# A two-layer attention and retention trunk: later query and key projection blocks held behind a score chunk by a one-element copy, and spread over heads 0 to 5

## The chip, the cores and the metric

The kernel runs on one core of a Trainium2 chip. A core has five engines that run side by side and meet at semaphores: TensorE for matrix products (PE in the profile, with its weight loads as PEld), VectorE (DVE), ScalarE (ACT), GpSimd (POOL), and SyncE (SP), which here issues nearly all DMA transfers. Each engine works through its own queue in order. The metric is device time of one execution in microseconds (us). Before the change the median of three runs is 2404.4 us (2401.87 to 2405.06).

## What is computed

Two layers, each a token mixer followed by a squared-ReLU MLP, both with a residual and a layer norm. The mixer has eight forgetting-attention heads of width 64 and four retention heads. The change lies in the attention heads alone:

```python
def fox_attention(q, k, v, log_f):
    c = jnp.cumsum(log_f.astype(jnp.float32), axis=1).transpose(0, 2, 1)
    ...
        scores = jnp.einsum('bqhd,bkhd->bhqk', q_i, k).astype(jnp.float32) * scale
        bias = c_i[..., :, None] - c[..., None, :]
        ...
        logits = jnp.where(causal, scores + bias, -jnp.inf)
        p = jax.nn.softmax(logits, axis=-1)
        return jnp.einsum('bhqk,bkhd->bqhd', p.astype(v.dtype), v)
```

There are 1024 tokens of width 1024. q, k and v are slices of one projection of the layer's input.

## The kernel before

Products that need full float32 accuracy are made of three: each operand is split into a high and a low part (`split`, L159: ScalarE makes the high part, VectorE the low one), and `mm3` (L229) issues low x high, high x low and high x high.

A layer runs in stages: value projections, retention, attention, output projection, and the two MLP products. Around the change:

**Projection blocks.** `project_qk(l, p, ...)` (L469) makes the queries and keys of a pair of heads, 2p and 2p+1. It yields four blocks: queries of tokens 0 to 511, queries of 512 to 1023, keys of 0 to 511, keys of 512 to 1023. A block is 8 x 3 matmuls of 128 rows by 512 columns into one PSUM bank of the pool `ps_mm` (two banks, tile `mm`), then an eviction (`ev`: one ScalarE and one VectorE instruction) and two stores to the DRAM buffers `q_d` or `k_d`. The generator yields after each k step and after each eviction, so a pair is 36 steps (`QK_STEPS`). Pair 0 is projected before the attention stage. Pairs 1 to 3, the twelve later blocks (called blocks 1 to 12 here: block 4 ends pair 1, block 8 pair 2, block 12 pair 3), are made inside it, by `rest()` (L699), followed by eight transposes of the retention output (`ret_transposes`).

**Attention.** A head has four steps qq = 0 to 3, each of two blocks of 128 query rows. `load(h)` (L498) fetches a head's queries `qs`, keys `ks` (four transfers) and values `vp` back from DRAM; `load_bias(h)` fetches the cumulative gate sums `ncb` (one buffer), and `bias` (POOL, `rel`) turns them into a bias for each step. `front` (L525) computes the scores of a step in chunks of up to 512 keys: two matmuls `qk<-ks,qs` into a bank of `ps_qk` (two banks), a causal mask added on the diagonal (`qk<-mbf,ibf`), then one VectorE instruction that adds the bias, writes `sc` and leaves the running row minimum `mx` (L547); after a row block's last chunk the exponential (ACT, L553), a reciprocal `ri` (DVE) and the scaling by it (POOL, L556). `back` (L560) transposes the probabilities (`tr<-cst,sc`, TensorE) and splits them into `pt` (ACT and DVE); `values` multiplies them with the head's values (`pv<-pt,vp`).

**Order.** In the program the front runs two steps ahead of the back (`DEPTH`), and `merge` interleaves back, front and n steps of `rest()`. n comes from `FILL[h]`, the number of steps a head gets, shared out in proportion to qq + 1. `need(p)` runs what is missing of pairs 1 to p at once. In the main loop step qq = 0 calls `need` (for odd heads) and `load(h+1)`; step qq = 1 calls `load_bias(h+1)`. This is not the order on the chip: the framework plays the whole program against a modelled timeline and gives each engine an instruction as soon as it counts it as ready. A projection block depends on nothing but its input, its weights and a free bank, so it may move far ahead of its place in the program. Once the order is made, an engine keeps to it and waits where something is late.

Of the kernel before, what the change touches and what calls it, by code (L numbers as in the profile page):

```python
# [46 lines left out]
PT_BUFS = 3  # L47
DEPTH = 2
LAG = 5
FILL = (18, 18, 18, 18, 18, 18, 4, 4)  # L50
QK_STEPS = 36


# [22 lines left out]
def hybrid_trunk(ctx: ExitStack, tc, x, w_in, w_out, w_ff1, w_ff2, ln1_g, ln1_b, ln2_g, ln2_b,  # L76
                 b_forget, ret_gn_g, cst_d, rope_d, out):
    nc = tc.nc
    A, V, G, PE, SP = nc.scalar, nc.vector, nc.gpsimd, nc.tensor, nc.sync
# [27 lines left out]
    def small(shape, tag, bufs=2):  # L107
        return sp.tile(shape, F32, tag=tag, name=nm(tag), bufs=bufs)
# [14 lines left out]
    def nm(s):  # L123
        uid[0] += 1
        return f"{s}_{uid[0]}"
# [18 lines left out]
    def tick():  # L144
        now = []
        for it in waiting:
            it[0] -= 1
            if it[0] <= 0:
                now.append(it)
        for it in now:  # L150
            waiting.remove(it)
        for it in now:
            it[1]()
# [5 lines left out]
    def split(hi, lo, src, scale=1.0):  # L159
        if scale == 1.0:  # L160
            A.copy(hi, src)  # L161
            V.tensor_tensor(lo, src, hi.bitcast(F32), op=ALU.subtract)  # L162
        else:
            A.mul(hi, src, scale)
            V.scalar_tensor_tensor(lo, src, scale, hi.bitcast(F32), op0=ALU.mult, op1=ALU.subtract)
# [58 lines left out]
    def weight(*key):  # L224
        while emitted[0] < min(ends[key[0]], place[key] + 1 + AHEAD):
            load_next()
        return loaded.pop(key)

    def mm3(ps, lhs, rhs, ks, first=True, last=True):  # L229
        n = len(ks)  # L230
        for i, k in enumerate(ks):
            for j, (a, b) in enumerate(((1, 0), (0, 1), (0, 0))):
                PE.matmul(ps, lhs(a, k), rhs(b, k), start=first and i == 0 and j == 0,  # L233
                          stop=last and i == n - 1 and j == 2)
# [231 lines left out]
            G.tensor_tensor(gt, gt, gn[:, 256 * r : 256 * r + 256], op=ALU.mult)  # L466
            defer(2, lambda tt=tt, vt=vt, gt=gt: core(tt, vt, gt))

    def project_qk(l, p, xT, pool=None):  # L469
        for name, dst, scale in (("fq", q_d, FD**-0.5), ("fk", k_d, 1.0)):  # L470
            w = weight(l, name, p)
            for hf in range(2):
                ps = ps_mm.tile([P, 512], F32, tag="mm", name=nm("mm"))
                for k in range(8):
                    mm3(ps, lambda a, k: w[a][:, k, :], lambda b, k: xT.at(b, k, 512 * hf, 512), [k], k == 0, k == 7)
                    yield
                if pool is not None and hf == 1:
                    ev = pool.tile([P, 2, 512], F32R, tag="ev2", name=nm("ev"), bufs=1)
                else:
                    ev = wp.tile([P, 2, 512], F32R, tag="ev", name=nm("ev"), bufs=1)  # L480
                split(ev[:, 0, :], ev[:, 1, :], ps, scale)
                for a in range(2):
                    SP.dma_start(dst[2 * p + a, :, :, 512 * hf : 512 * hf + 512].rearrange("s d n -> d s n").bitcast(F32),
                                 ev[64 * a : 64 * a + 64].bitcast(F32))
                tick()
                yield
# [5 lines left out]
            transpose_in(mr, t, tt, groups=1)  # L492
            yield

    def attention(pool, mixes, fill, need, take):
        pv, heads, sums, rels, pvq, outs = {}, {}, {}, {}, [], {}

        def load(h):  # L498
            qs = pool.tile([P, S], F32R, tag="qs", name=nm("qs"), bufs=2)
            SP.dma_start(qs.bitcast(F32), q_d[h].rearrange("s d n -> (s d) n").bitcast(F32))  # L500
            ks = []
            for part in range(2):
                kt = pool.tile([P, S], F32R, tag=f"ks{part}", name=nm("ks"), bufs=2)
                for a in range(2):
                    SP.dma_start(kt[64 * a : 64 * a + 64].bitcast(F32), k_d[h, part].bitcast(F32))
                ks.append(kt)
            vp = pool.tile([P, NT, P], F32R, tag="vp", name=nm("vp"), bufs=2)
            SP.dma_start(vp.bitcast(F32), v_d[:, h].rearrange("(t p) s d -> p t (s d)", p=P).bitcast(F32))
            heads[h] = (qs, ks, vp)
# [15 lines left out]
        def front(h, qq, probs):  # L525
            qs, ks, _ = heads[h]
            n = 256 * (qq + 1)
            rel = rels.pop((h, qq))
            for rb in (2 * qq, 2 * qq + 1):
                ne = (rb + 1) * P  # L530
                sc = pool.tile([P, n], F32, tag=f"sc{qq}", name=nm("sc"), bufs=2)
                mx = None
                nw = max(ne, 256)
                cw = 512 if nw <= 512 or nw % 256 == 0 else nw // 2
                for c0 in range(0, nw, cw):
                    w = min(cw, nw - c0)
                    we = min(w, ne - c0)
                    ps = ps_qk.tile([P, 512], F32, tag="qk", name=nm("qk"))
                    last = c0 + w == nw
                    for part in range(2):  # L540
                        PE.matmul(ps[:, 0:w], qs[:, rb * P : rb * P + P], ks[part][:, c0 : c0 + w],  # L541
                                  start=part == 0, stop=part == 1 and not last)
                    if last:
                        o = rb * P - c0
                        PE.matmul(ps[:, o : o + P], ibf, mbf, start=False, stop=True)
                    m2 = small([P, 1], "mx", 6)
                    V.tensor_tensor_reduce(out=sc[:, c0 : c0 + we], in0=ps[:, 0:we], in1=rel[:, c0 : c0 + we], scale=-1.0,  # L547
                                           scalar=BIG if mx is None else mx, op0=ALU.add, op1=ALU.min, accum_out=m2)
                    mx = m2
                    if not last:  # L550
                        yield
                sm = small([P, 1], "sm", 4)
                A.activation(sc[:, 0:ne], sc[:, 0:ne], AF.Exp, bias=mx, scale=-1.0, accum_out=sm)  # L553
                ri = small([P, 1], "ri", 4)
                V.reciprocal(ri, sm)  # L555
                G.tensor_scalar(sc[:, 0:ne], sc[:, 0:ne], ri, 1.0, op0=ALU.mult, op1=ALU.mult)  # L556
                probs.append(sc)
                yield
# [61 lines left out]
        def fronts(st, probs):  # L620
            h, qq = st
            return (2 * (1 + qq // 2), front(h, qq, probs))
# [8 lines left out]
        for i, st in enumerate(steps):  # L631
            h, qq = st
            n = fill(h, qq)
            if h + 1 < FH:
                if qq == 0:
                    if h % 2 == 1:
                        need((h + 1) // 2)
                    load(h + 1)
                if qq == 3 - DEPTH:
                    load_bias(h + 1)  # L640
            gens = [(2 * (qq + 1), back(h, qq, probs[st]))]
            if i + DEPTH < len(steps):
                nx = steps[i + DEPTH]
                gens.append(fronts(nx, probs[nx]))
            if n:
                gens.append((n, take(n)))
            merge(gens)
            if i + DEPTH + 1 < len(steps):
                bias(*steps[i + DEPTH + 1])
# [3 lines left out]
    def layer(l, xT, nxt):  # L653
# [42 lines left out]
        mix = {}  # L696
        mr = Tokens(act, "act")
        with tc.tile_pool(name=f"p2_{l}", bufs=1, reuse_waits="tile") as pool:
            def rest():  # L699
                for p in range(1, FH // 2):  # L700
                    yield from project_qk(l, p, xT, pool)
                yield from ret_transposes(mr, pool)

            work = rest()

            done = [0, 0.0]

            def fill(h, qq):
                done[1] += FILL[h] * (qq + 1) / 10
                return max(0, int(done[1]) - done[0])  # L710

            def take(n):
                for _ in range(n):
                    done[0] += 1
                    next(work, None)
                    yield

            def need(p):
                while done[0] < QK_STEPS * p:
                    done[0] += 1  # L720
                    next(work, None)

            attention(pool, mix, fill, need, take)
            for _ in work:
                pass

# [10 lines left out]
        with tc.tile_pool(name=f"p3_{l}", bufs=1, reuse_waits="tile") as outer:  # L737
# [3 lines left out]
            with tc.tile_pool(name=f"p3a_{l}", bufs=1, reuse_waits="tile") as pool:  # L741
# [42 lines left out]
                ps = banks(1) + banks(0)  # L784
# [9 lines left out]
                for tt in range(NT):  # L794
                    ps = bank()
# [193 lines left out]
    class Operands:  # L989
# [36 lines left out]
        def take(self, p, j):  # L1026
            self.ahead(self.todo.index((p, j)) + 1 + E_AHEAD)
            return self.ready.pop((p, j))
# [118 lines left out]
    xT = Tokens(act, "act")  # L1147
    for l in range(L):
        nxt = Tokens(act, "act") if l + 1 < L else None
        layer(l, xT, nxt)  # L1150
        xT = nxt
# [27 lines left out]
```

## Time and profile before

| | us |
|---|---|
| median of three runs | 2404.4 |
| the profiled execution, its time | 2406.83 |
| the profiled execution, span of its instructions | 2404.8 |
| attention stage, layer 0: first score matmul to last value matmul | 313.8 to 518.7 |
| attention stage, layer 1 | 1504.7 to 1707.7 |
| granted TensorE clock, mean of the run | 0.997 |

The span is the time from the first to the last instruction; 2.0 us of the execution lie around it. In rows of groups the columns are line, engine, operation, destination and source tiles, shapes and count, then busy time and mean duration, then idle time before the instructions and what ended it. In a timeline row the first two numbers are start and duration in us, the number after x counts merged instructions, and brackets give idle time before the row and its releaser. Window rows give the stretch, its length, and for each engine busy us and instruction count, then the granted clock, the DMA share and GB/s. A matmul's end is modelled: a matmul shown as busy may be held up.

### The profile page before, as it was taken

How to read it: one execution, taken by the hardware profiler on the slowest of the kernel's cores; microseconds unless marked ns; L12 is line 12 of the kernel's file. 1: busy time of each engine (PE TensorE's matmuls, PEld its weight loads, DVE VectorE, ACT ScalarE, POOL GpSimd, SP SyncE). 2: the span in 40 equal slices, each digit the busy share in tenths (PEclk: the TensorE clock that was granted, in tenths of full speed). 3: DMA queues.
4: the chain of work that ended last, by engine and by line, in shares of the span. 5: the costliest groups of instructions: out<-in, count | busy, mean ns of one | idle time of the engine just before them, and what ended most of it. 6: DMA issues, size and time to landing. Idle time of an engine off the chain costs nothing.

```text
span 2404.8 us, 32463 instructions
## 1 busy us (share of the span) xinstructions
PE 2361.1 (98%) x11888; PEld 1983.0 (82%) x11888; DVE 1510.0 (63%) x2703; ACT 1015.2 (42%) x1556; POOL 337.0 (14%) x469
## 2 busy tenths in 40 slices
PE   8999999999999999999999999999999999999997
PEld 8888887887888888888898888888888888888886
DVE  4655447854876667665755554588467766676557
ACT  3222246735544553434321212477274444543331
POOL 0223223500000000000202322244000000000003
PEclk9999999999999999999999999999999999999999
DMA  7465676433364458667555567664334544586664
GB/s 233 165 220 207 216 212 183 123 119 113 109 221 148 145 188 310 211 210 223 179 164 187 209 212 231 182 177 116 132 101 147 199 164 148 213 294 214 196 194 145
DMA packets 243807, 442.47 MB, mean 184 GB/s; under 512 B 26032, under 2 KB 128432, under 8 KB 235456
## 3 DMA queue, kind: packets, MB, share of 16 engines
q1 hardware_dynamic: 241344, 432.01, 55.2%
q10 hardware_dynamic: 2304, 8.39, 0.9%
q8 instruction: 94, 1.54, 0.3%
q14 instruction: 65, 0.53, 0.1%
HBM read 301.85 MB, written 138.48 MB: 183 GB/s over the span
## 4 chain that ended last, share of the span: by engine, by line
PE 88%; DMA 4%; DVE 4%; ACT 1%; issue 1%; SPq 0%; POOL 0%; DVEq 0%; ACTq 0%; POOLq 0%
PE mm L233 17%; PE qk L233 11%; PE qk L860 9%; PE tr L1070 7%; PE pv L1070 7%; PE pv L860 7%; PE qk L1070 5%; PE mm L1070 5%; PE mm L860 5%; PE tr L860 4%; PE tr L569 2%; PE qk L541 2%; PE pv L591 2%; DMA q_d<-ev 1%; PE pv L233 1%
## 5 line engine op out<-in xcount | busy, mean ns | idle before, releaser
L162 DVE TENSOR_TENSOR elo<-est,ehi 128x1024 fp32r<-128x1024 f32 x216 | 261.2, 1222 | 180.3 <-ACT ehi L161 179.4
L161 ACT CAST ehi<-est 128x1024 fp32r<-128x1024 f32 x216 | 226.7, 1054 | 343.4 <-PE pv L1070 127.5
L233 PE MATMUL mm<-whi,act 128*128 128x512 f32 (+1 forms) x608 | 187.9, 375 | 0.9 <-DVE act L162 0.5
L233 PE MATMUL qk<-whi,act 128*128 128x512 f32 (+1 forms) x608 | 186.6, 373 | 0.8 <-DVE act L162 0.8
L860 PE MATMUL qk<-xop,whi 128*128 128x512 f32 x608 | 187.3, 389 | 0.0
L161 ACT CAST whi<-wst 128x512 fp32r<-128x512 f32 (+1 forms) x140 | 115.9, 830 | 165.8 <-PE qk L233 36.0
L286 POOL TENSOR_SCALAR sd<-mv 128x1 f32<-128x1 f32 x15 | 13.9, 928 | 1211.4 <-DVE mv L283 1211.0
L860 PE MATMUL pv<-xop,whi 128*128 128x512 f32 x512 | 157.7, 389 | 0.0
L162 DVE TENSOR_TENSOR wlo<-wst,whi 128x512 fp32r<-128x512 f32 (+1 forms) x140 | 132.0, 946 | 39.2 <-ACT whi L161 38.6
L860 PEld LDWEIGHTS qk<-xop,whi 128*128 128x128 f32 x608 | 114.2, 188 | 23.6
L162 DVE TENSOR_TENSOR pt<-tr,pt 128x512 fp32r<-128x512 f32 (+1 forms) x160 | 99.7, 631 | 46.5 <-ACT pt L161 45.8
L233 PEld LDWEIGHTS mm<-whi,act 128*128 128x128 f32 x608 | 112.6, 192 | 19.7 <-ACT whi L161 0.8
L591 PE MATMUL pv<-pt,vp 128*128 128x256 f32 (+1 forms) x640 | 127.5, 302 | 0.2
L233 PE MATMUL mm<-act,whi 128*128 128x512 f32 x384 | 125.9, 396 | 0.0
L233 PEld LDWEIGHTS qk<-whi,act 128*128 128x128 f32 x608 | 110.3, 189 | 18.7 <-DVE act L162 1.0
L553 ACT ACTIVATE sc<-sc,mx 128x128 f32<-128x128 f32 (+7 forms) x128 | 99.4, 777 | 51.9 <-DVE mx L547 44.4
L860 PE MATMUL mm<-xop,whi 128*128 128x512 f32 x384 | 118.6, 390 | 1.5 <-DVE xop L162 1.5
L860 PE MATMUL qk<-xop,wlo 128*128 128x512 f32 x304 | 118.6, 390 | 0.0
L556 POOL TENSOR_SCALAR sc<-sc,ri 128x128 f32<-128x128 f32 (+7 forms) x128 | 96.8, 762 | 136.7 <-DVE ri L555 104.8
L161 ACT CAST pt<-tr 128x512 fp32r<-128x512 f32 (+1 forms) x160 | 85.8, 541 | 70.0 <-PE tr L569 67.9
L233 PE MATMUL mm<-wlo,act 128*128 128x512 f32 (+1 forms) x304 | 113.7, 374 | 0.7 <-DVE wlo L162 0.7
L860 PEld LDWEIGHTS pv<-xop,whi 128*128 128x128 f32 x512 | 96.1, 188 | 20.0
(278 smaller groups left out, 5942.8 us busy)
## 6 DMA issues: line engine op xcount, KB each, us to landing
est<-h_d SPq DMA_DIRECT2D x224, 256.0 KB, 3.6
wst<-in_w_ff_dram SPq DMA_DIRECT2D x76, 512.0 KB, 4.3
wr<-in_w_ff_dram SPq DMA_DIRECT2D x32, 1024.0 KB, 5.1
t_d<-ts SPq DMA_DIRECT2D x32, 1024.0 KB, 4.2
h_d<-hs SPq DMA_DIRECT2D x32, 1024.0 KB, 5.5
est<-t_d SPq DMA_DIRECT2D x128, 256.0 KB, 4.0
h_d<-rest SPq DMA_DIRECT2D x32, 768.0 KB, 5.7
est<-in_w_ff_dram SPq DMA_DIRECT2D x96, 256.0 KB, 4.8
```

Source lines behind the costliest of these rows:

```text
L161: A.copy(hi, src)
L162: V.tensor_tensor(lo, src, hi.bitcast(F32), op=ALU.subtract)
L233: PE.matmul(ps, lhs(a, k), rhs(b, k), start=first and i == 0 and j == 0, stop=last and i == n - 1 and j == 2)
L286: G.tensor_scalar(sd, mv[:, :, 1], EPS, 1.0, op0=ALU.add, op1=ALU.mult)
L541: PE.matmul(ps[:, 0:w], qs[:, rb * P : rb * P + P], ks[part][:, c0 : c0 + w], start=part == 0, stop=part == 1 and not last)
L553: A.activation(sc[:, 0:ne], sc[:, 0:ne], AF.Exp, bias=mx, scale=-1.0, accum_out=sm)
L556: G.tensor_scalar(sc[:, 0:ne], sc[:, 0:ne], ri, 1.0, op0=ALU.mult, op1=ALU.mult)
L569: PE.transpose(tr[:, 2 * i + rb, :], probs[rb][:, j * P : j * P + P], ident)
L591: PE.matmul(ob[:, c + f * P : c + 256], vp[:, js[i], :], pt[b][:, 2 * i + f : 2 * i + 2, :], start=qq % 2 == 0 and jp == 0 and n == 0 and ...
L860: PE.matmul(ps, ops[p][a][:, k, :], right[p][b][:, k, :], start=first and k == 0 and n == 0, stop=last and k == 3 and n == 2, skip_group_c ...
L1070: PE.matmul(ps, ops[x_][:, 0, i * P : i * P + P], ops[y][:, 1, :], start=first and n == 0, stop=last and n == 2, skip_group_check=True)
```

## The change

Nine of the twelve later blocks, from block 4 on, get a new first instruction: VectorE copies one element of the newest `mx` into the block's PSUM bank. The block's first matmul overwrites the bank, so the value is of no use; but the matmuls now come after the copy, and the copy after the score chunk that made `mx`. `FILL` is given anew, so that the steps are spread over heads 0 to 5 without a run of `need` that makes half a pair at once. `load(h+1)` and `need` move from step 0 to step 1 of the head before.

```diff
-FILL = (18, 18, 18, 18, 18, 18, 4, 4)
+FILL = (34, 18, 18, 18, 18, 6, 3, 3)
+FREE = 3
...
-    def project_qk(l, p, xT, pool=None):
+    def project_qk(l, p, xT, pool=None, held=None):
...
                 ps = ps_mm.tile([P, 512], F32, tag="mm", name=nm("mm"))
+                if held is not None:
+                    held(ps)
...
                     mx = m2
+                    latest[0] = mx
...
             if h + 1 < FH:
-                if qq == 0:
+                if qq == 3 - DEPTH:
                     if h % 2 == 1:
                         need((h + 1) // 2)
                     load(h + 1)
-                if qq == 3 - DEPTH:
                     load_bias(h + 1)
...
+            latest, count = [None], [0]
+
+            def held(ps):
+                count[0] += 1
+                if count[0] > FREE:
+                    V.tensor_copy(ps[0:1, 0:1], latest[0][0:1, :])
...
-                    yield from project_qk(l, p, xT, pool)
+                    yield from project_qk(l, p, xT, pool, held)
```

What the scheduler makes of it is the same in both layers. In TensorE's queue blocks 1 to 3 end right before the first score matmul in both kernels. Before the change blocks 4 to 12 then stand among the scores of heads 0, 1 and 2, and block 12 ends there. After it they stand among the scores of heads 1 to 5, about two blocks a head, mostly as runs of 15 to 18 matmuls. The work of each engine is the same but for the nine copies a layer.

The first place is TensorE's queue at the start of attention in layer 0. Names with `qk` are score banks, `tr` the bank of the first transposes, `mm` a projection block. Before, around the fourth score chunk:

```order
L541 MATMUL qk_2933<-ks_2878,qs_2876 128x512
L541 MATMUL qk_2933<-ks_2881,qs_2876 128x512
L545 LDWEIGHTS ibf
L545 MATMUL qk_2933<-mbf,ibf 128x128
L569 MATMUL tr_2954<-cst,sc_2908 128x128
L569 MATMUL tr_2954<-cst,sc_2896 128x128
L569 MATMUL tr_2954<-cst,sc_2908 128x128
L233 MATMUL mm_3356<-act_165,wlo_2971 128x512
L233 MATMUL mm_3356<-act_166,whi_2970 128x512
L233 MATMUL mm_3356<-act_165,whi_2970 128x512
```

After, the same chunk and the same transposes (lines are numbered by the new file):

```order
L544 MATMUL qk_2933<-ks_2881,qs_2876 128x512
L548 LDWEIGHTS ibf
L548 MATMUL qk_2933<-mbf,ibf 128x128
L544 MATMUL qk_2963<-ks_2878,qs_2876 128x320
L544 MATMUL qk_2963<-ks_2881,qs_2876 128x320
L544 MATMUL qk_2974<-ks_2878,qs_2876 128x320
L544 MATMUL qk_2974<-ks_2881,qs_2876 128x320
L548 LDWEIGHTS ibf
L548 MATMUL qk_2974<-mbf,ibf 128x128
L573 MATMUL tr_2954<-cst,sc_2908 128x128
L573 MATMUL tr_2954<-cst,sc_2896 128x128
L573 MATMUL tr_2954<-cst,sc_2908 128x128
```

The projection matmuls that stood between score chunks are gone; two more score chunks stand ahead of the first transposes, and no projection matmul follows until 34 score matmuls have been issued.

The second place is TensorE's queue at head 6, whose keys are made by block 12. Before, at head 6's first score chunk (`ks_4686`), block 12 lies some 370 rows back:

```order
L545 MATMUL qk_4805<-mbf,ibf 128x128
L569 MATMUL tr_4757<-cst,sc_4572 128x128
L569 MATMUL tr_4757<-cst,sc_4604 128x128
L569 MATMUL tr_4757<-cst,sc_4572 128x128
L569 MATMUL tr_4757<-cst,sc_4604 128x128
L591 MATMUL pv_4867<-pt_4699,vp_4296 128x256
L591 MATMUL pv_4867<-pt_4698,vp_4296 128x128
L591 MATMUL pv_4867<-pt_4699,vp_4296 128x128
L541 MATMUL qk_4856<-ks_4686,qs_4684 128x256
```

After, block 12 (`mm_4593`) ends here:

```order
L544 MATMUL qk_4703<-ks_4399,qs_4394 128x320
L548 LDWEIGHTS ibf
L548 MATMUL qk_4703<-mbf,ibf 128x128
L234 MATMUL mm_4593<-act_306,wlo_3752 128x512
L234 MATMUL mm_4593<-act_307,whi_3751 128x512
L234 MATMUL mm_4593<-act_306,whi_3751 128x512
L595 MATMUL pv_4633<-pt_4580,vp_4066 128x256
```

and head 6's first score matmuls (`ks_4743`) stand 53 rows further on: 12 score matmuls, 3 masks, 10 transposes and 24 value matmuls lie between.

```order
L544 MATMUL qk_4814<-ks_4399,qs_4394 128x512
L548 LDWEIGHTS ibf
L548 MATMUL qk_4814<-mbf,ibf 128x128
L595 MATMUL pv_4876<-pt_4761,vp_4402 128x256
L595 MATMUL pv_4876<-pt_4760,vp_4402 128x256
L595 MATMUL pv_4876<-pt_4761,vp_4402 128x256
L544 MATMUL qk_4865<-ks_4743,qs_4741 128x256
L544 MATMUL qk_4882<-ks_4743,qs_4741 128x256
```

So a distance of most of three heads has become a distance of 49 short matmuls. For heads 2 and 4 the same distance holds the next projection block as well.

The third place is SyncE's queue at the loads of head 6. Before, the last stores of block 12 (`ev_4679`) lie before the loads of head 4 (`qs_4005`); after, they stand directly ahead of the loads of head 6's keys:

```order
L511 DMA vp_4402<-v_d 128x8x128
L503 DMA qs_4741<-q_d 128x1024
L516 DMA ncb_4751<-c_d 128x1024
L486 DMA k_d<-ev_4584 64x2x512 x2
L486 DMA k_d<-ev_4736 64x2x512 x2
L212 DMA wst_5746<-in_w_out_dram 128x2x512
L508 DMA ks_4743<-k_d 64x1024 x2
L508 DMA ks_4746<-k_d 64x1024 x2
```

The key loads must wait until the two stores ahead of them have landed.

More of the change, by code (lines that the diff above doesn't have):

```diff
@@ L493, in ret_transposes, with attention @@
             yield
-    def attention(pool, mixes, fill, need, take):
+    def attention(pool, mixes, fill, need, take, latest):
         pv, heads, sums, rels, pvq, outs = {}, {}, {}, {}, [], {}
@@ L721, in need @@
                     next(work, None)
-            attention(pool, mix, fill, need, take)
+            attention(pool, mix, fill, need, take, latest)
             for _ in work:
```

## The prediction

> **What bounds the kernel now.** I read the page's busy times first, then the windows of the attention stage, then the groups inside one window, and last single waits.
>
> ```profile
> span 2404.8 us, 32463 instructions
> PE 2361.1 (98%) x11888; PEld 1983.0 (82%) x11888; DVE 1510.0 (63%) x2703; ACT 1015.2 (42%) x1556; POOL 337.0 (14%) x469
> ```
>
> TensorE is the bound nearly everywhere. The change leaves its work as it is, so it can only win or lose time in which TensorE waits. Three windows of the attention stage:
>
> ```profile
> 319.00:394.00 75.00, 74.78 (x426) 62.35 (x425) 45.27 (x120) 38.38 (x78) 25.21 (x35) 1.00 0.57 168
> 399.00:449.00 50.00, 45.32 (x322) 38.25 (x322) 45.39 (x139) 39.34 (x87) 27.63 (x39) 0.97 0.66 183
> 1590.00:1640.00 50.00, 46.42 (x338) 38.70 (x337) 47.67 (x146) 41.78 (x91) 29.46 (x41) 1.00 0.70 196
> ```
>
> From 319 to 394 the projection blocks fill every gap: TensorE is busy throughout, VectorE (third pair of numbers) for 45 of 75 us. From 399 to 449 they are used up; VectorE is busy for 45.4 of 50 us and sets the pace. So does it in layer 1 from 1590 to 1640. How much TensorE loses there its busy time understates, since a matmul held up counts as busy. I count the work instead:
>
> ```profile
> L591 PE MATMUL pv<-pt,vp 128*128 128x256 f32 (+1 forms) x117 | 23.3, 308 | 0.0
> L541 PE MATMUL qk<-ks,qs 128*128 128x512 f32 (+4 forms) x72 | 20.1, 369 | 0.8 <-DVE mx L547 0.8
> L569 PE MATMUL tr<-cst,sc 128*128 128x128 f32 x105 | 17.6, 285 | 4.0 <-POOL sc L556 1.9 <-DVE pt L162 1.7
> ...
> L541 PE MATMUL qk<-ks,qs x72: 277/368/628, 399.6 to 448.3; 128*128 128x512 f32 x24, 128*128 128x256 f32 x18, 128*128 128x320 f32 x12, 128*128 128x448 f32 x12
> ```
>
> The pace of matmuls that wait for nothing:
>
> ```profile
> 400.68 0.72 PE L591 MATMUL pv<-pt,vp 128*128 128x256 f32 x4
> 401.24 0.60 PE L569 MATMUL tr<-cst,sc 128*128 128x128 f32 x4
> 401.60 0.70 PE L591 MATMUL pv<-pt,vp 128*128 128x256 f32 x4
> ...
> 413.37 0.63 PE L541 MATMUL qk<-ks,qs 128*128 128x512 f32 x2
> 413.83 0.40 PE L591 MATMUL pv<-pt,vp 128*128 128x256 f32 x2
> ```
>
> Four value matmuls and four transposes take 0.92 us from start to start (400.68 to 401.60), 0.115 each; two score matmuls of 512 columns take 0.46, 0.23 each, and a narrower one its share. 222 value matmuls and transposes then come to 25.5 us. The 72 score matmuls have 28,416 columns (the last six, not in the row, are 384 wide), 55.5 times 512, so 12.8 us; the 24 masks, at an estimated 0.05 each, to 1.2. That is 39.5 us of work in 50: **10.5 us are lost** in three heads, a quarter more than the work. Layer 1's window holds a little more work (338 matmuls against 322), so by the same pace about 8.5 us are lost. These 19 us are what spreading the blocks can win.
>
> **The change, part by part.** Its own nine copies a layer are cheap. The nearest row is a one-element copy out of PSUM:
>
> ```profile
> L979 DVE COPY wr<-qk x32: 134/138/147, 78.9 to 1464.5; 1x1 f32<-1x1 f32 x32
> ```
>
> At 0.14 us each they add 1.3 us a layer to a VectorE that, once spread, has slack; behind a copy only the next evictions wait, and TensorE's first matmul of the block. I take 0, at most 1.3.
>
> *What is won.* A block is 24 matmuls of 512 columns at 0.23, 5.5 us; nine of them come to 50 us of filling for heads 1 to 5. Four heads of attention are 53 us of TensorE work by the count above, so heads 1 to 5 hold some 103 us. VectorE has 15.1 us a head (45.4 over three), 61 for four, and beside them the blocks' own work:
>
> ```profile
> L162 DVE TENSOR_TENSOR wlo<-wst,whi 128x1024 fp32r<-128x1024 f32 x4 | 4.9, 1220 | 0.0
> ...
> L162 DVE TENSOR_TENSOR ev<-mm,ev 128x512 fp32r<-128x512 f32 x5 | 3.4, 690 | 5.7 <-ACT ev L161 5.7
> ```
>
> Nine evictions and some six weight splits are 14 us, 75 in all. TensorE is the bound again on the mean. But the queue has the fillers in runs of 15 to 18, some 4 us, while score and transpose banks let VectorE keep only about four instructions in hand, about 2.5 us (four of 0.55 to 0.63 by the mean durations below). Between two runs VectorE still sets the pace at times.
>
> ```profile
> L162 DVE TENSOR_TENSOR pt<-tr,pt 128x512 fp32r<-128x512 f32 (+1 forms) x30 | 18.5, 629 | 0.4 <-ACT pt L161 0.3
> ...
> L547 DVE CUSTOM_DVE_ANT_0 sc<-qk,rel 128x512 f32<-128x512 f32 (+5 forms) x25 | 13.8, 552 | 3.0 <-PE qk L545 2.8 <-PE tr L569 0.2
> ```
>
> I leave 0.35 us lost for each of the nine intervals, 3.1 a layer, and take **6.4 us won a layer** (9.5 on the mean less 3.1). Ends: all of 9.5, or 4.
>
> *What the start loses.* Now the projection matmuls between head 0's first scores are gone. In the trace of before this is the start:
>
> ```profile
> 313.81 0.40 PE L541 MATMUL qk<-ks,qs 128*128 128x256 f32 x2
> ...
> 319.04 0.20 POOL L515 TENSOR_SCALAR ref<-ncb 128x4 f32<-128x4 f32 x1 [11.57 <-DMA ncb<-c_d]
> 319.33 0.48 POOL L522 TENSOR_SCALAR rel<-ncb,ref 128x256 f32<-128x256 f32 x1
> 319.79 0.84 POOL L556 TENSOR_SCALAR sc<-sc,ri 128x128 f32<-128x128 f32 x2
> ...
> 321.04 0.50 PE L569 MATMUL tr<-cst,sc 128*128 128x128 f32 x3
> ```
>
> The first transposes need both of head 0's first probability blocks, scaled by POOL, and POOL waits for head 1's `ncb` until 319.04. In the new order one scaling stands ahead of that wait and one behind, so the transposes still start near 321, 7.2 us after the first score. Until then TensorE has six score chunks, about 2.1 us of work by the paces above: 5.1 us idle. The further work up to block 4 is 8.7 us (10.8, counted in the queue, less 2.1); a quarter more for VectorE's pace would be 2.2, but VectorE begins that stretch with nothing in arrears, so I take 0.9. **6 us lost a layer**; ends 3 (the bias lands 3 us sooner) and 8 (the quarter and refilling in full).
>
> *What the heads 2, 4 and 6 lose.* A head's keys pass from a block's eviction through two stores and four loads. The start of the stage shows the whole chain, since head 0's keys come straight from pair 0:
>
> ```profile
> 298.55 0.59 ACT L161 CAST ev<-mm 128x512 fp32r<-128x512 f32 x1 [5.14 <-DMA k_d<-ev]
> 299.17 0.69 DVE L162 TENSOR_TENSOR ev<-mm,ev 128x512 fp32r<-128x512 f32 x1 [5.03 <-ACT ev L161]
> 299.89 1.24 SPq L483 DMA_DIRECT2D k_d<-ev  x2
> ...
> 304.92 5.11 SPq L505 DMA_DIRECT2D ks<-k_d  x8
> ```
>
> From the eviction at 298.55 to the first score at 313.81 it took 15.3 us, with other loads beside it. Layer 1 gives 14.0:
>
> ```profile
> 1490.69 0.59 ACT L161 CAST ev<-mm 128x512 fp32r<-128x512 f32 x1 [5.09 <-DMA k_d<-ev]
> ...
> 1504.73 0.40 PE L541 MATMUL qk<-ks,qs 128*128 128x256 f32 x2
> ```
>
> The best case goes by the fastest landing of a key load and the usual one of a store:
>
> ```profile
> DMA to landing us min/median/max: 3.6/6.7/8.7
> ...
> k_d<-ev SPq DMA_DIRECT2D x12, 256.0 KB, 3.3
> ```
>
> Eviction 1.3, two stores issued at 0.6 each and the second landing 3.3 after its issue (3.9), four loads at 0.6 with the last landing 3.6 after its issue (5.4): 10.6 us. Against this stands TensorE's work between block 12 and head 6. By the paces above the 49 matmuls come to 3.9 us (34 value matmuls and transposes) and 2.6 (12 scores, 3 masks), 6.5; at VectorE's pace, a quarter more, 8.2. **Head 6 stalls for 5 us a layer**: chain 13.2, a little under the two measured since fewer loads run beside it; ends 1.5 (10.6 less 8.2, rounded down) and 7.1 (15.3 less 8.2). Everything behind that score matmul in TensorE's queue waits with it, and VectorE runs dry. Between blocks 4 and 8 and heads 2 and 4 lie 12.4 and 12.7 us of work, a projection block in it; with a quarter more on the attention part about 14. There I take 0.5 us each, **1 us a layer**, ends 0 and 3. Loads moved by one step are in this chain. For odd heads the keys are long in DRAM; they have a step less, but heads 1 to 5 are longer now by their blocks. I take 0 for them.
>
> *The clock.* Short waits already cost one drop of it in layer 0:
>
> ```profile
> 416.50:420.00 3.50, 1.64 (x13) 1.27 (x12) 1.93 (x8) 1.81 (x4) 3.50 (x5) 1.00 1.06 335
> 420.30:423.70 3.40, 3.40 (x16) 2.76 (x15) 2.39 (x7) 2.75 (x9) 2.81 (x4) 0.54 1.06 247
> ```
>
> TensorE was busy for 1.64 of 3.5 us, and for the next 3.4 the granted clock was 0.54: about 1.6 us lost. Idle spells of 5.1 us (start) and 5 us (head 6) can do the same, twice a layer; part of it falls where VectorE sets the pace. **1 us lost a layer**, ends 0 and 3. The Trainium skill, "TensorE: Matmul & The Clock Gate", Part 1, says that the clock halves after an idle window of about 3.4 us and holds until a busy one; the row agrees with 0.54, though TensorE was not fully idle before it. By that rule each drop is 1.7 us and both would come, 3.4 a layer in place of 1.
>
> **The sum**, a layer: -6.4 + 6 + 5 + 1 + 1 = +6.6 us, for two layers +13.2. The profiled execution of before took 2406.8 us (2404.8 of span and 2.0 around it) and would take 2420; the median of the runs is 2.4 lower, so I predict **2418 us**, 0.5% slower. With all terms at their good ends -9.5 + 3 + 1.5 = -5 a layer, 2394; at their bad ends -4 + 8 + 7.1 + 3 + 3 = +17, 2439.
>
> **The rivals.** *Spreading wins.* The chain lands at its best, 10.6 us, the start costs 3.5, and 9 of the 9.5 are won: -9 + 3.5 + 1.5 = -4 a layer, 2396. For it: from 319 to 394 filled heads lose next to nothing (74.78 of 75 busy); in the middle of the stage fewer loads run beside the chain than at its start. Against it: the median landing of key loads is 6.7, not 3.6, and the fillers come in long runs.
>
> A page speaks for a part of this case: the Trainium skill, "DMA: Bandwidth & Descriptors", section "Anatomy of one DMA", gives about 2.0 us fixed plus bytes over 436 GB/s for a transfer on the GpSimd path. That would be 2.6 us for 256 KB here, and an estimate by it makes the chain 8.9 us and the stall 0.7; the forecast would fall to 2409. The rows (3.3 and 6.7 on SyncE's path) do not agree, so it moves nothing above.
>
> *Even.* Start and stall cost as much as the filling wins, each near 6 to 8 a layer: 2404. It needs a stall of about 2 and a start of about 4.
>
> *Nothing moves.* If the holds had no effect the time would stay; the queue speaks against it, so this adds little to the case above.
>
> *Runs starve VectorE.* If after each run of fillers the pipe of scores, exponentials and transposes has to fill anew, an interval loses 1 us and not 0.35, 9 a layer in place of 3.1; with the rest as forecast this gives +12 a layer, 2429. It decides where VectorE's slack in heads 1 to 5, 28 us by the count above, is less than what it idles: 1.6 us in each of nine runs (4.1 less 2.5), and about 1.5 to refill behind each.
>
> **How the numbers follow.** Forecast (2405 to 2428): 0.52. Spreading wins: 0.20. Even: 0.15. Runs starve VectorE: 0.13. The range leaves out a tenth at either end: **2396 to 2431**; the forecast's own is the one given. A measurement can tell about 0.2% here, 4.8 us. Slower by more: the forecast less its lowest part, and the last case, 0.62. Faster by more: 0.19. Within: 0.19.
>
> **What would show it.** Right: TensorE idle for 4 us or more a few us after head 0's first score, ended by POOL's `sc`; a TensorE wait of 3 to 7 us at head 6's first score, with `ks<-k_d` in the chain ahead of it; VectorE below 0.85 busy in heads 2 to 4; more windows with a clock of 0.5. Wrong: head 6 starts without a wait, or the windows of heads 1 to 5 show TensorE held up again with VectorE at 0.95; then the won term, not the stall, decides. The two stages are 204 us long on the mean (313.8 to 518.7 and 1504.7 to 1707.7); the sum says 210.6, and 199 or less would refute it.

## The result, and the profile after

| | before | after |
|---|---|---|
| median of four, us | 2404.73 (2401.87 to 2405.29) | 2430.11 (2428.69 to 2435.13) |
| profiled execution, its time | 2406.83 | 2431.21 |
| span | 2404.8 | 2429.5 |
| granted clock, mean | 0.997 | 0.992 |
| attention stage, layer 0: first score to last value matmul | 313.8 to 518.7 | 313.3 to 531.9 |
| attention stage, layer 1 | 1504.7 to 1707.7 | 1513.6 to 1735.8 |

The change makes the kernel slower: ratio 1.0106, 95% interval 1.0093 to 1.0118. Layer 1's first score comes 8.9 us later than before; that is layer 0's share, and the other 16 us fall in layer 1.

The page of after, its span, its busy times and the group of the score matmuls:

```profile
span 2429.5 us, 32458 instructions
...
PE 2369.3 (98%) x11888; PEld 1989.8 (82%) x11888; DVE 1502.0 (62%) x2721; ACT 1013.3 (42%) x1556; POOL 338.0 (14%) x469
...
L544 PE MATMUL qk<-ks,qs 128*128 128x512 f32 (+4 forms) x384 | 111.4, 378 | 13.4 <-DMA ks<-k_d 11.0
```

TensorE has the same 11888 matmuls. New is the end of the last row: the scores waited 13.4 us, 11.0 of them for a head's keys. TensorE's waits by cause in each stage (us in total, times, the longest), layer 0 and then layer 1 of after, and last the longest of layer 0 before:

```profile
PE qk L544 <- DMA ks<-k_d: 5.2, 3, 3.2
PE tr L573 <- DVE pt L163: 3.2, 6, 0.8
PE tr L573 <- POOL sc L560: 2.7, 1, 2.7
...
PE qk L544 <- DMA ks<-k_d: 5.8, 3, 3.8
PE tr L573 <- DVE pt L163: 3.3, 6, 0.8
PE tr L573 <- POOL sc L560: 2.8, 1, 2.8
PE tr L259 <- DMA rl<-r_d: 1.3, 1, 1.3
...
PE tr L569 <- POOL sc L556: 1.9, 2, 1.4
PE tr L569 <- DVE pt L162: 1.7, 2, 0.9
```

Before has no wait for `ks`. The wait for `sc` is the start; of the waits for `ks` two stand at head 6 (4.8 us in layer 0, 5.4 in layer 1), and the third, of 0.35, at the first score. In the timeline of layer 0 the start is this, first TensorE and then POOL:

```profile
317.54 0.23 PE L548 MATMUL qk<-mbf,ibf 128*128 128x128 bf16 x1
320.48 0.55 PE L573 MATMUL tr<-cst,sc 128*128 128x128 f32 x3 [2.70 <-POOL sc L560]
...
319.19 0.20 POOL L518 TENSOR_SCALAR ref<-ncb 128x4 f32<-128x4 f32 x1 [3.04 <-DMA ncb<-c_d]
319.49 0.48 POOL L525 TENSOR_SCALAR rel<-ncb,ref 128x256 f32<-128x256 f32 x1
319.94 0.48 POOL L560 TENSOR_SCALAR sc<-sc,ri 128x256 f32<-128x256 f32 x1
```

The scores are issued by 317.54; the transposes come at 320.48, 7.2 us after the first score, because the second scaling stands behind the bias of head 1. And head 6, TensorE's timeline and then the chain of waits (start, us, what):

```profile
449.22 0.61 PE L595 MATMUL pv<-pt,vp 128*128 128x256 f32 x3
453.05 0.47 PE L544 MATMUL qk<-ks,qs 128*128 128x256 f32 x2 [3.21 <-DMA ks<-k_d]
455.14 0.55 PE L544 MATMUL qk<-ks,qs 128*128 128x256 f32 x1 [1.62 <-DMA ks<-k_d]
...
442.69 0.48 ACT ev L162
443.19 0.44 DVE ev L163
...
443.92 3.17 DMA k_d<-ev
447.10 0.48 SPq L508
447.63 0.59 SPq L508
448.27 0.59 SPq L508
448.90 6.11 DMA ks<-k_d
```

From the eviction of block 12 (it starts at 442.59) to the score matmul that needs the last key load (455.14) it is 12.5 us. TensorE's two waits for keys are 4.8 of them; in the other 7.7 it had work, but for a wait of 0.8 for `pt`. Layer 1 gives 13.1 and 5.4 us.

At both waits the clock falls. Windows, columns as in the prediction; the granted clock is the third number from the end:

```profile
317.50:320.50 3.00, 0.30 (x4) 0.12 (x2) 0.89 (x6) 0.44 (x2) 1.21 (x4) 1.00 1.04 402
320.90:324.30 3.40, 3.40 (x16) 2.92 (x15) 2.33 (x8) 2.22 (x6) 2.48 (x5) 0.50 0.51 136
449.80:453.00 3.20, 0.04 (x1) 0.00 (x0) 1.28 (x4) 1.24 (x2) 2.11 (x2) 1.00 1.00 274
454.00:460.80 6.80, 5.21 (x18) 3.70 (x19) 2.17 (x10) 2.50 (x7) 1.93 (x3) 0.50 1.07 327
...
1519.00:1525.80 6.80, 5.01 (x21) 4.53 (x22) 3.16 (x10) 3.47 (x8) 4.72 (x8) 0.50 0.79 262
1655.50:1665.70 10.20, 8.36 (x30) 6.45 (x31) 3.77 (x16) 4.17 (x11) 3.18 (x5) 0.50 1.05 278
```

27.2 us at half speed in the two stages, against one drop of 3.4 before.

To compare heads I count the loss as the prediction does, but instruction by instruction: the distance from one TensorE start to the next, less the pace of the first (0.227 us for 512 columns, 0.12 for 256, 0.11 for 128, 0.06 for a mask), added up from a head's first score to the next head's. A wait and a half clock both show in it; the work does not. In us, layer 0 / layer 1:

| kernel | head 0 | heads 1 to 4 | heads 5, 6 | head 7 | stage |
|---|---|---|---|---|---|
| before | 1.2 / 1.8 | 9.9 / 7.3 | 3.3 / 3.5 | 4.6 / 4.6 | 19.0 / 17.1 |
| after | 6.7 / 7.6 | 5.3 / 5.4 | 11.9 / 13.7 | 4.2 / 5.2 | 28.2 / 31.8 |

After loses 9.2 and 14.7 us more, 23.9 of the span's 24.7. (The stages themselves are 219 and 222 us long; 4.5 us of that are 20 matmuls of the output projection, which now run ahead of the last value matmul, so the stage's length alone overstates.)

### The profile page after: what moved, and what is told of

The parts are those of the page before. It is cut to its first block, busy times and chain, and to the rows that moved or that the text cites. A ratio compares the mean times of both kernels' runs of the same rounds, so it can differ in the third digit from the quotient of the medians.

```text
span 2429.5 us, 32458 instructions
## 1 busy us (share of the span) xinstructions
PE 2369.3 (98%) x11888; PEld 1989.8 (82%) x11888; DVE 1502.0 (62%) x2721; ACT 1013.3 (42%) x1556; POOL 338.0 (14%) x469
## 4 chain that ended last, share of the span: by engine, by line
PE 79%; DMA 4%; DVE 3%; ACT 1%; issue 1%; SPq 0%; POOL 0%; DVEq 0%; ACTq 0%; POOLq 0%
PE mm L234 12%; PE qk L870 8%; PE tr L1080 7%; PE pv L870 7%; PE qk L234 7%; PE pv L1080 7%; PE qk L1080 5%; PE mm L1080 5%; PE mm L870 5%; PE tr L870 4%; PE qk L544 2%; PE tr L573 2%; PE pv L595 2%; PE tr L234 1%; PE pv L234 1%
## 5 line engine op out<-in xcount | busy, mean ns | idle before, releaser
L544 PE MATMUL qk<-ks,qs 128*128 128x512 f32 (+4 forms) x384 | 111.4, 378 | 13.4 <-DMA ks<-k_d 11.0
```

## The experiments

Each edit is against after; ratios are to the kernel before on the same chip, with 95% intervals.

**1. Without the hold (no_hold).** The table of steps and the moved loads stay, no copy is made.

```diff
-FREE = 3
+FREE = 99
```

> The changed kernel with no block held (the count from which blocks are held set to 99): the new table and the moved loads stay, the nine copies a layer go. The queue of TensorE then has blocks 4 to 12 back among the scores of heads 0 to 2. Theory (start and head 6): the 25 us come from where the hold puts the blocks, so this runs like the kernel before, 2405 us (2400 to 2410). Rival (the moved loads and the new table cost): it stays near 2430. Rival (the copies and the long runs of projection matmuls starve VectorE): also near 2405, so this run does not tell it from the theory.

2407.08 us, ratio 1.0006 (0.9996 to 1.0015). The stages lose 18.6 and 21.0 us, against 19.0 and 17.1 before; the one drop of the clock, which before has in layer 0, falls in layer 1 here. The new table and the moved loads alone move nothing.

**2. The hold alone (hold_alone).** The copies are added to before, with its table and its loads where they were.

```diff
-FILL = (34, 18, 18, 18, 18, 6, 3, 3)
+FILL = (18, 18, 18, 18, 18, 18, 4, 4)
...
-                if qq == 3 - DEPTH:
+                if qq == 0:
                     if h % 2 == 1:
                         need((h + 1) // 2)
                     load(h + 1)
+                if qq == 3 - DEPTH:
                     load_bias(h + 1)
```

> The copies on nine blocks are the only change: FILL and the place of the loads are those of before. Blocks 4 to 12 then stand in three bursts of two to three blocks, at heads 1, 3 and 5, and block 12 ends 6.4 us of work ahead of head 6. Theory (the waits at the start and at head 6 come from the holds, whatever the table): both waits are there, of 2 to 3 and 3 to 6 us, and since bursts leave heads 2 and 4 thin the time is 2432, in 2427 to 2440. Rival (the table set the stall by placing block 12 late): no wait on keys at head 6, 2418 or less.

2437.36 us, ratio 1.0125 (1.0108 to 1.0142). Both waits are there. Head 6 in its timeline:

```profile
457.38 0.55 PE L544 MATMUL qk<-ks,qs 128*128 128x256 f32 x1 [5.07 <-DMA ks<-k_d]
459.33 0.55 PE L544 MATMUL qk<-ks,qs 128*128 128x256 f32 x1 [1.40 <-DMA ks<-k_d]
```

The stall comes from the hold under either table, since `need` runs half a pair just ahead of the head that reads it. With 1, this shows the cause: the copies. Whether the new table softens them (1.0106) is not clear, since the two intervals overlap.

**3. The start alone (free_five).** Blocks 4 and 5 are free too, and run among head 0's first scores as before.

```diff
-FREE = 3
+FREE = 5
```

> Five blocks a layer run free, not three: blocks 4 and 5 stand among head 0's scores again, seven are held. Head 6 still follows block 12 by 6.5 us of work. Theory (start and head 6): TensorE's wait at the first transposes goes (2.7 us of idle and the slow clock behind it, 5.5 us a layer), but heads 1 and 2 have a stretch without filler in exchange, about 3 us a layer; the stall at head 6 stays, about 5 us idle a layer: 2424 us (2418 to 2428). Rival (copies and runs starve VectorE): two copies of nine less, the same runs in heads 2 to 5: 2425 to 2430, with no change in the start's share.

2420.15 us, ratio 1.0054 (1.0037 to 1.0071). The wait for `sc` is gone and no drop of the clock follows it; head 0 loses 2.6 and 2.9 us, heads 5 and 6 still 11.9 and 12.4. The start is worth 1.0106 less 1.0054, 12.5 us, 6 a layer; by the count 8.8 of them lie in head 0 itself.

**4. The end alone, first try (early_blocks).** The blocks end in head 4.

```diff
-FILL = (34, 18, 18, 18, 18, 6, 3, 3)
+FILL = (34, 26, 26, 24, 4, 4, 3, 3)
```

> The table of steps is (34, 26, 26, 24, 4, 4, 3, 3): nine copies as before, but block 12 ends in head 4, and 32 us of TensorE work lie between it and head 6 in place of 6.5 (30 between block 8 and head 4). Theory (start and head 6): the wait for the keys of head 6 and the slow clock behind it go, 9 us a layer; head 5 is without filler in exchange, about 3 us a layer: 2418 us (2412 to 2422), and no idle time of TensorE before a score that a key load ends. Rival (copies and runs starve VectorE): nine copies and nine runs are still there, 2428 to 2432.

2421.02 us, ratio 1.006 (1.0045 to 1.0075). The time is in the range given, but not for the reason given. The wait for keys is gone, and another is in its place, in heads 4 and 5:

```profile
430.64 0.72 PE L544 MATMUL qk<-ks,qs 128*128 128x512 f32 x2
433.72 0.66 PE L259 MATMUL tr<-cst,rl 128*128 128x128 f32 x4 [2.36 <-DMA rl<-r_d]
```

The table counts the eight transposes of the retention output behind the 108 projection steps. 110 steps by the end of head 3 pull the first of them into heads 4 and 5, and their load `rl` arrives late.

**5. Both, first try (free_five_early).**

```diff
-FILL = (34, 18, 18, 18, 18, 6, 3, 3)
-FREE = 3
+FILL = (42, 20, 20, 20, 10, 4, 3, 3)
+FREE = 5
```

> Both: five blocks free and the table (42, 20, 20, 20, 10, 4, 3, 3), so block 12 ends 26 us of TensorE work ahead of head 6. Theory (start and head 6): both losses go, about 25 us, and what is left is two stretches without filler (15 and 27 us of work) in place of the one of 43 us before: 2405 us (2399 to 2410), level with the kernel before. Rival (copies and runs starve VectorE): seven copies and runs remain, 2420 or more. If spreading is worth what was forecast for it (6.4 us a layer) in full, below 2398.

2430.37 us, ratio 1.0096 (1.0081 to 1.0111): a miss by 25 us. Start and key wait are gone, the table gives 112 steps by head 4, and the waits for `rl` (7.8 us in layer 0) cost as much as both: heads 5 and 6 lose some 17 us in each layer. The chain of waits and the transposes that it ends in:

```profile
428.84 4.86 DMA k_d<-ev
433.70 0.02 issue
433.71 9.12 DMA rl<-r_d
...
442.97 0.63 PE L259 MATMUL tr<-cst,rl 128*128 128x128 f32 x4 [4.06 <-DMA rl<-r_d]
```

`rl` takes the one buffer `ev2` that the last projection block's eviction also uses, so its load must wait for block 12's stores, as the keys do; then 256 KB take 9.1 us to land among the loads of the next head.

**6. The end alone, without the new wait (early_tail).** 108 steps by the end of head 3, none in heads 4 and 5, and the transposes in heads 6 and 7, where before has them.

```diff
-FILL = (34, 18, 18, 18, 18, 6, 3, 3)
+FILL = (34, 26, 26, 22, 0, 0, 4, 4)
```

> As after, with FILL (34, 26, 26, 22, 0, 0, 4, 4): block 12 ends some 21 us of work ahead of head 6 and the retention transposes stay in heads 6 and 7; the start keeps its wait (three free blocks). Theory: head 6's key wait and its clock drops go, and no new wait for the retention output comes; the start stays at 5 to 6 us a layer and one drop; 2413, in 2408 to 2418, below the 2421 of early_blocks. Rival (the late heads without filler lose more than the wait did): 2420 or above, with the excess of heads 5 to 7 as large as in early_blocks and no load in front of it.

2407.18 us, ratio 0.9996 (0.9987 to 1.0005), below the range given. Heads 5 and 6 lose 4.0 and 4.6 us; TensorE's only waits there (428 to 470) are three for `mx`:

```profile
PE qk L544 <- DVE mx L550: 1.0, 3, 0.5
```

So the new table is worth 1.1%, 26 us by the medians and 22 by the spans (2429.5 less 2407.4). By the count 17.0 us of this lie in heads 5 and 6, 8.5 a layer: that is the stall at head 6 with what follows it, where the prediction had 5 and a part of its 1 for the clock. The other 5 us come mostly from heads 1 to 4 and head 7, whose steps this table changes too.

**7. Both, second try (five_early_tail).**

```diff
-FILL = (34, 18, 18, 18, 18, 6, 3, 3)
-FREE = 3
+FILL = (42, 22, 22, 22, 0, 0, 4, 4)
+FREE = 5
```

> Five blocks are free, seven held, and FILL is (42, 22, 22, 22, 0, 0, 4, 4): all blocks end in head 4, about 21 us of TensorE work ahead of head 6, and the transposes of the retention output stay in heads 6 and 7, as before the change. Theory (waits at the start, for head 6's keys, and for the retention output are what costs; with all three gone only the gain of spreading is left, 2 to 5 us a layer): TensorE has no single wait over 2 us in heads 0 to 5, one clock drop at most, and the time is 2400, in 2394 to 2405. Rival (spreading in runs of fillers is itself worth nothing, or costs; VectorE sets the pace between runs): 2406 to 2415, with many waits below 1 us and none long.

2406.38 us, ratio 0.9994 (0.9985 to 1.0004). No wait for keys or `rl` is left, but head 0 loses 6.1 and 4.0 us, and layer 0 has a drop of the clock at 322.7, so the sum of 3 and 6 does not come out. Seen alone this fits the rival; run 10 goes against it.

**8 and 9. The clock (dead_work, dead_work_long).** Dead matmuls of 512 columns, behind block 12 and held by a copy like it, stand a few rows ahead of head 6's first score, where TensorE waits. Nobody reads their result.

```diff
+            def dead(n):
+                if n:
+                    ps = ps_mm.tile([P, 512], F32, tag="mm", name=nm("dead"))
+                    V.tensor_copy(ps[0:1, 0:1], latest[0][0:1, :])
+                    for i in range(n):
+                        PE.matmul(ps, xT.at(0, 0, 0, 128), xT.at(0, 0, 0, 512), start=i == 0, stop=i == n - 1)
...
                     yield from project_qk(l, p, xT, pool, held)
+                dead(20)
```

> As after, with 20 matmuls of 512 columns (4.6 us by 0.23 each) more, whose result nobody reads, ahead of head 6's first score matmul, where TensorE waits 4.0 to 4.8 us and then 1.6 us for the keys. The chain of the keys is as long as before, so by its length the waiting is only replaced by dead work. Theory (the clock: 6.8 and 10.2 us at half speed behind these waits are the larger part of what the forecast missed): no window of half speed behind head 6's start, key wait below 2 us, and the time falls by 4 to 8 to 2424, in 2421 to 2427. Rival (VectorE sets the pace behind the wait anyway, so the half speed is free): the drops go and the time stays at 2429 to 2432. Second rival (the dead work doesn't lie in the wait): 2434 or more.

2432.05 us, ratio 1.0102 (1.008 to 1.0123): inconclusive. The key wait shrinks to 0.9 and 1.4 us, but the transposes of `rl` now wait 2.0 and 2.3 us behind it, and the half speed comes all the same, 3.4 us in each layer. With 32 in place of 20:

> dead_work with 32 matmuls in place of 20: 7.3 us of work whose result nobody reads, enough for the keys and for the retention load that in dead_work came 2 us behind them and brought the half speed back. After loses 11.9 and 13.7 us in heads 5 and 6 of the two layers. Theory (5.2 and 5.8 of that are the keys, the half speed behind them costs 2.1 and 3.5): no half speed at head 6, no wait over 1 us there, and the loss is 7.3 of dead work and some 4 more, 11.3; so the time stands 3 us below after in all, a ratio to before of 1.0093, in 1.008 to 1.0105. Rival (the waits alone count and the half speed lies in VectorE's time): the dead work is longer than the waits, and the ratio is 1.012 or more.

2425.0 us, ratio 1.0082 (1.0066 to 1.0097). Now nothing waits, and the clock stays at 1.00 behind head 6's start (timeline, then a window):

```profile
448.42 7.44 PE L714 MATMUL dead<-act 128*128 128x512 f32 x32
455.70 0.61 PE L544 MATMUL qk<-ks,qs 128*128 128x512 f32 x2
456.16 0.23 PE L548 MATMUL qk<-mbf,ibf 128*128 128x128 bf16 x1
456.20 0.48 PE L544 MATMUL qk<-ks,qs 128*128 128x256 f32 x2
...
452.00:460.00 8.00, 7.95 (x47) 6.21 (x45) 2.54 (x11) 2.69 (x7) 2.06 (x2) 1.00 0.75 204
```

Heads 5 and 6 lose 3.7 us in either layer, and 7.3 of dead work make 11.0, where after loses 11.9 and 13.7. VectorE is about as idle beside the dead work as beside the wait (busy for 2.04 of 7.60 us from 448.4 here, for 1.28 of 5.30 from 449.8 in after), so it is TensorE's idleness alone that is gone. In after the waits there were 4.8 and 5.4 us. Had they been all, 7.3 in their place would have cost 2.5 and 1.9 us more; instead it cost 0.9 and 2.7 less. So 3.4 and 4.6 us were what follows the wait; the half-speed windows themselves account for 2.1 and 3.5 of it (each instruction's distance beyond its pace, up to once that pace). The ratio, 1.0082 against 1.0106, falls the same way, though the two intervals touch.

**10 and 11. A version of both (free_five_early_tail, five_tail_thin).** Five free blocks with the table of run 6, and a variant that reaches a little into head 4.

```diff
-FILL = (34, 18, 18, 18, 18, 6, 3, 3)
-FREE = 3
+FILL = (34, 26, 26, 22, 0, 0, 4, 4)
+FREE = 5
```

> Five blocks are free, and FILL is that of early_tail, (34, 26, 26, 22, 0, 0, 4, 4). early_tail lost 7.4 and 7.5 us of TensorE time in head 0, free_five 2.6 and 2.9; elsewhere early_tail lost 11.3 and 11.9. Theory (the start and the tail add up, since each is a wait of its own): 2407.2 less 4.7 a layer, 2398, in 2393 to 2402, faster than both kernels. Rival (the start's price is not the blocks ahead of it but comes with any thinning of the front, as five_early_tail with 6.1 and 4.0 in head 0 may show): 2404 to 2408.

2398.36 us, ratio 0.997 (0.996 to 0.9981): faster than both kernels. Heads 1 to 4 lose 3.8 and 4.1 us, heads 5 and 6 3.9 and 4.1, and the clock does not drop in either stage. TensorE's waits in layer 0:

```profile
PE mm L234 <- DVE ev L163: 1.5, 1, 1.5
PE qk L544 <- DVE mx L550: 0.7, 2, 0.5
PE tr L573 <- POOL sc L560: 0.3, 1, 0.3
```

The largest, 1.5 us at 320, is a held block that waits for the eviction of a free one: two banks for five free blocks. Run 7 has the same wait (1.4) behind one for `sc` of 0.7, and a drop of the clock behind both.

The two removals do not quite add up: runs 3 and 6 together would give a ratio of 0.9944, and 0.997 was measured. Seen from run 6, which still has the start's wait, the start is worth 0.9996 less 0.997, some 6 us, and not 12.5.

The variant has `FILL = (34, 24, 24, 22, 4, 0, 4, 4)`:

> The same with FILL (34, 24, 24, 22, 4, 0, 4, 4): the blocks reach into head 4 a little more evenly, block 12 ends 18 us of work ahead of head 6. Theory (VectorE's pace in the heads without filler is what remains): up to 2 us below free_five_early_tail, in 2392 to 2402. Rival (18 us are too little for the keys or the first retention load, which wait behind block 12's stores): a wait on ks or rl in head 5 or 6 and 2404 or more.

2402.84 us, ratio 0.999 (0.9981 to 0.9999): no better. Head 4 now loses 3.0 us (a wait of 0.9 for `mx` among them) where run 10 loses 1.1, but head 0 loses less, so the count explains only 1 us of the 3.9 between the two profiled spans; the rest stays open. No load is late.

## Why the prediction was right in its sign and half in its size

Forecast 2418, measured 2430.1: slower, as forecast, but by 25 us and not 13. That is outside the forecast's own 2405 to 2428 and inside the whole range (2396 to 2431) by 1 us, and this is in part luck: the gain and the clock missed by more than the sum shows, and the start and heads 2 and 4, taken 6 us too high over both layers, hid some of it. Term by term, a layer, from the counts of after less before:

| term | forecast | measured, layer 0 / 1 |
|---|---|---|
| won by spreading | -6.4 | -4.6 / -1.9 (heads 1 to 4) |
| start of head 0, without the clock | +6 | +4.2 / +3.8 |
| heads 2 and 4 | +1 | 0: no wait for keys there |
| stall at head 6 | +5 | +4.8 / +5.4 |
| clock | +1 | +3.4 / +5.5 |
| left over | | +1.4 / +1.9 |
| sum | +6.6 | +9.2 / +14.7 |

The clock's line is the loss within the half-speed windows, counted as in run 9; 1.4 us of before's own drop are in the first line, as in the forecast. What is left over has in layer 1 a wait of 1.3 us for `rl` in head 7. The 2.6 us more that layer 0 wins than layer 1 were lost before in one place, head 4 (4.4 against 1.7 us), where that kernel's own drop lies.

**The start** was right in mechanism: the transposes came 7.2 us after the first score, as said, ended by POOL's scaling, and run 3 took the loss away. The idle stretch is 2.7 us and not the 5.1 forecast, and the sign that I named, 4 us or more, did not show: small waits stretch the score chunks to 317.54, and the rest of the loss lies in them. Of 6 us, 4 are this and 1.3 to 2.0 the clock.

**The stall at head 6** was right in size. The chain measured 12.5 us (13.1 in layer 1) where I took 13.2, and TensorE's time beside it 7.7 where I took 8.2. Run 6, which puts more work in between, removed it with all copies in place. What I did not see is that `rl` stands in the same chain.

**The clock** was a mis-sized term. I took 1 us a layer because "part of it falls where VectorE sets the pace". At head 6 it does not: the row 454.00 to 460.80 has VectorE busy for 2.17 of 6.80 us, so it waits for TensorE behind the stall. (At the start in layer 0 it is busy for 2.33 of 3.40.) The drops were also longer than the one that I had a row for, 6.8 and 10.2 us against 3.4; at head 6 the second key load's wait of 1.6 us lies at their beginning. Run 9 shows that some 3.4 and 4.6 us followed the wait at head 6. The Trainium skill, "TensorE: Matmul & The Clock Gate", Part 1, has the clock judged in free-running windows of 3413 ns; the spells of 3.4, 6.8 and 10.2 agree with it, and the 3.4 us a layer that the prediction worked out beside the sum (layer 0 has 3.4, layer 1 5.5) was nearer than my 1. The same part of the Trainium skill asks for an idle window of about 3.4 us; ahead of the drop at the start the row shows a gap of 2.70, so here less was enough.

**The gain** was the other mis-sized term, by 3 us a layer. The step that failed is "0.35 us lost for each of the nine intervals". Heads 1 to 5 without the stall (run 9) lose 6.8 us in layer 0, 0.75 an interval, in good part one pause of 0.4 to 1.1 a head, for `pt` or `ri`, among the runs of fillers. Of the 6.8, 2.4 were lost in heads 1 and 2 before too, where I had counted nothing from a row that showed TensorE busy for 74.78 of 75 us: a matmul held up counts as busy, as the prediction itself warns. VectorE did get its slack:

```profile
327.10:428.90 101.80, 99.34 (x624) 84.79 (x624) 70.13 (x204) 61.27 (x131) 39.57 (x55) 1.00 0.58 162
```

70 of 102 us, 0.69, below the 0.85 that the prediction named. So the rival in which runs starve VectorE had the size half right (0.75 lies between its 1 and my 0.35) but not the reason, since VectorE had slack; that its 2429 was nearly met is chance, for the clock added as much as the runs. That spreading can win is shown by run 10: with both waits away, and the blocks spread over heads 0 to 3, it gains 0.3%.

That the clock and the gain together make the difference is arithmetic from counts; run 9 tests the clock's part at head 6, and no run took the clock's drop at the start away by itself. Open is also why run 7 lost 2.9 us more than run 10 in head 0 and 3.5 in heads 1 to 4 (both layers together); the two differ in the table alone. In heads 1 to 4 run 7 has waits for `pt` of 1.4 us a layer that run 10 does not have, which is most of the 3.5, but not why they come.

## What to carry to other kernels

Work without dependencies that a scheduler runs early is often the cover of a load chain behind it; before holding it back, measure the chain from its last write to its first read (12.5 and 13.1 us here) and keep at least that much of the waiting engine's own work between. The stalls of TensorE here, 2.7 and 2.8 us at the start, 4.8 and 5.4 at head 6, cost their own length and 1.3 to 3.5 us of half clock besides, so count both. And look for every reader behind the held work's buffer: here the retention loads stood behind the same eviction and took the stall over when the keys were out of the way.

## What the runs showed of the hardware

Half-clock spells came in steps of 3.4 us. They lasted for two or three steps at head 6, where a second wait of 1.6 us lay at their beginning (6.8 us in layer 0, 10.2 in layer 1), although TensorE shows as busy for 5.21 of the 6.80 and 8.36 of the 10.20; and for two at the start in layer 1, where the spell had begun before the wait of 2.80 us ended. Pairs of shorter waits went with a spell of 3.4 us too: 0.92 and 1.99 us in run 8, 0.67 and 1.40 in run 7; with 0.33 and 1.47 in run 10 there was none. Filling waits of 4.8 and 5.4 us with 7.3 us of useless matmuls left the kernel no slower, and by the medians faster (1.0106 to 1.0082, intervals that touch). And in run 5 a 256 KB load took 9.1 us to land beside a head's other loads (DMA share 1.03 meanwhile), and 2.6 in a calmer place of the same stage (0.36):

```profile
458.04 2.58 DMA rl<-r_d
...
465.77 7.33 DMA rl<-r_d
```
